# Decoder layer with 32 experts: order of experts computed at the last ranks, a 32-slot second expert, first down weights ahead of its gates, another tail

## The chip, the cores and the metric

The kernel runs on one core of a Trainium2 chip. The metric is the device time of one execution in microseconds (us), the median of the runs. The core's engines are PE (TensorE, matrix products into PSUM), DVE (VectorE), ACT (ScalarE), POOL (GpSimd) and SP (SyncE, here the queue that issues nearly all loads). They run side by side and wait for each other by semaphores; every engine works off its own instructions in the order in which they were written.

## The reference, cut to what matters

```python
def reference(x, positions, w_in, ..., w_gate_up, b_gate_up, w_down, b_down, ln2_g, ln2_b):
    mixed = attention(x) @ w_o[l]                      # two head groups, 512 tokens, width 1024
    x = layer_norm(DN_ALPHA * x + mixed, ln1_g[l], ln1_b[l])
    y = moe_ffn(x, w_router[l], b_router[l], w_gate_up[l], b_gate_up[l], w_down[l], b_down[l])
    x = layer_norm(DN_ALPHA * x + y, ln2_g[l], ln2_b[l])

def moe_ffn(...):
    logits = (xt @ w_router + b_router).astype(jnp.float32)
    top_logit, top_idx = lax.top_k(logits, TOP_K)      # 4 of 32 experts for each token
    gates = jax.nn.softmax(top_logit, axis=-1)
    ...
        h = xb @ w_gate_up[e] + b_gate_up[e]           # 1024 -> 2048
        act = (up + 1.0) * (gate * jax.nn.sigmoid(gate * SWIGLU_ALPHA))
        y = act @ w_down[e] + b_down[e]                # 1024 -> 1024
        return y * g[:, None]
```

All is float32. The weights of all 32 experts (12 MiB each, 384 MiB in all) are read whatever the router says.

## The kernel before

**Stages.** Projection and attention run over four blocks of 128 tokens (`PLAN`, `ORDER`, a table written by hand). A finished block goes through the `tasks`: output projection (`out_proj`), `norm` (layer norm, row block stored to `x1d`), `logits`, `logits2` (router) and `ranks`. `ranks` gives each token its place among the tokens of each expert (`rk1`). Then `moe` goes over 32 positions.

**Positions and kinds.** `KINDS` gives each position a kind: H has room for 128 tokens, L for 64, T for 32; G is H and T together, D is H and L. An H tile is split into two halves (`convert`: `whi` on ACT, `wlo` on DVE, lines 246 and 247) and multiplied in three passes (`mm3`, lines 253 to 255); the landed buffer is free again once it is converted. L and T use the landed tile itself (`mm_parts`, line 1261), with two or four pieces of the array side by side; the buffer is free once it has been multiplied. Positions 0 and 1 are both H and always hold experts 0 and 1, their weights have fixed addresses; which expert stands at a later position is computed (`permute`): experts by their count of tokens, the fullest in the positions with most room. The table `v` of experts is read into a register on SP (`expert_reg`) for the addresses of positions 2 and up.

**Weights.** `Stream` loads tiles of 1 MiB through SP into a ring of 11 buffers, 12 from the start of `moe`: eight gate/up tiles and four down tiles for each position. The work, and with it the order of the loads, is gates(0), gates(1), down(0), gates(2), down(1), and so on. A tile is loaded as soon as the program has released a buffer (`Stream.ahead`); when the engine that reads that buffer is late, SP waits there, and so does everything that it has to issue behind it.

**Start of `moe`.** The last call of `ranks` makes the matmul that selects the rows of expert 0 (`first_xT`: eight pairs, one on the gathered rows `xg` and one on the last block `x1`, lines 1165 and 1166). During gates(0) `permute` runs in pieces between the tiles (`between`), and so do the parts of the bias (`bias_part`). Rows for position 1 are gathered by POOL behind the loads of the biases, and turned to columns (`load_xT`) behind gates(0) and its `swiglu`.

**Tail.** Results of positions 0 to 29 are scattered to `yd`. Positions 30 and 31 are kept in SBUF and added by a matmul with the gates (`tail_kept`). While gates(31) run, `tail_y` loads the eight tiles of `yd` (two for each block of 128 tokens), ahead of the four down tiles of position 31. `tail_sum` adds four rows with their gates on DVE (line 1543), `tail_first` starts the sum of a block in PSUM (lines 1561 and 1551), `tail` ends with the layer norm and eight stores. In `down(31)` the blocks' `tail_first` stand between the four quarters.

## Time and profile before

| | us |
|---|---|
| median of 3 runs | 1410.86 |
| lowest and highest run | 1407.32, 1410.98 |
| the profiled execution, its own time | 1411.22 |
| span of its instructions | 1409.4 |

The span is read in four stretches: projection and attention (0 to about 314), the start of `moe` (314 to about 420), the row of experts (420 to about 1300) and the tail (1300 to the end). For each of them the rate of the DMA engines tells whether the weights come at full rate, and the waits tell who holds up whom. The engines' busy shares over the whole span (PE 91%) say little here, since they are means over stretches with different limits.

### The profile page before, as it was taken

To read this page: it belongs to the slowest core of one execution; us is meant where nothing else is said; L and a number is where in the kernel's file an instruction comes from. 1 tells how busy PE (TensorE), PEld (TensorE's weight loads), DVE (VectorE), ACT (ScalarE), POOL (GpSimd) and SP (SyncE) were. 2 spreads that over 40 slices of the span, in tenths; PEclk is the share of its full clock that TensorE was granted. 3 is DMA by queue.
4 is the path that set the end of the run, shared out by engine and by line. 5 is a ranking of instruction groups with operands and counts; after the bars stand their busy time and mean duration, and the time that the engine had idled before them with its cause. 6 is when DMAs were issued, how large, how long until landed. Compare 5 with 4: busy or idle time off the path is not lost.

```text
span 1409.4 us, 18034 instructions
## 1 busy us (share of the span) xinstructions
PE 1277.2 (91%) x6543; PEld 807.6 (57%) x6543; DVE 734.6 (52%) x1285; ACT 560.8 (40%) x829; POOL 162.8 (12%) x183
## 2 busy tenths in 40 slices
PE   6989697968999989999899999999999999999952
PEld 5767686856756435456554444647766556654310
DVE  4453654467946335335633523638855638752054
ACT  3442543335635224333622413536753627542201
POOL 2232100002001000010110000101011101000003
PEclk9999898979999999999999999999999999999887
DMA  9101730276799999999999998999999999999961
GB/s 336 72 1 60 273 146 34 90 281 239 290 375 415 416 418 418 413 413 416 417 417 415 416 353 349 417 417 416 417 417 417 417 413 414 415 415 408 407 261 65
DMA packets 92508, 464.70 MB, mean 330 GB/s; under 512 B 10226, under 2 KB 11426, under 8 KB 58624
## 3 DMA queue, kind: packets, MB, share of 16 engines
q1 hardware_dynamic: 82160, 435.42, 76.4%
q0 software_dynamic: 8000, 19.18, 3.8%
q10 hardware_dynamic: 2256, 8.91, 1.7%
q8 instruction: 53, 0.87, 0.2%
q14 instruction: 39, 0.32, 0.1%
HBM read 445.59 MB, written 25.03 MB: 334 GB/s over the span
## 4 chain that ended last, share of the span: by engine, by line
PE 55%; DMA 26%; DVE 9%; ACT 4%; issue 2%; POOL 1%; SPq 0%; ACTq 0%; DVEq 0%; POOLq 0%
PE acc L1261 14%; DMA raw<-in_w_down_dram 14%; DMA raw<-in_w_gate_up_dram 9%; PE acc L253 8%; PE acc L254 8%; PE acc L255 8%; DVE wlo L247 3%; PE acc L1267 2%; DMA yr<-yd 1%; PE ip L253 1%; PE ip L254 1%; PE ip L255 1%; DMA yr<-x1d 1%; PE po L667 1%; ACT whi L246 1%
## 5 line engine op out<-in xcount | busy, mean ns | idle before, releaser
L247 DVE TENSOR_TENSOR wlo<-raw,whi 128x1024 fp32r<-128x1024 f32 (+3 forms) x361 | 421.3, 1217 | 141.4 <-ACT whi L246 139.3
L246 ACT CAST whi<-raw 128x1024 fp32r<-128x1024 f32 (+3 forms) x361 | 358.4, 1046 | 175.4 <-DMA raw<-in_w_down_dram 81.1
L1261 PE MATMUL acc<-raw,xTs 128*64 128x512 f32 (+1 forms) x1280 | 266.8, 605 | 14.7 <-DMA raw<-in_w_gate_up_dram 14.6
L253 PE MATMUL acc<-whi,xTh 128*128 128x512 f32 x448 | 182.2, 407 | 0.7 <-ACT xTh L261 0.7
L254 PE MATMUL acc<-wlo,xTh 128*128 128x512 f32 x448 | 177.6, 396 | 0.6 <-DVE wlo L247 0.6
L255 PE MATMUL acc<-whi,xTl 128*128 128x512 f32 x448 | 177.4, 396 | 0.0
L1261 PEld LDWEIGHTS acc<-raw,xTs 128*64 128x64 f32 (+1 forms) x1280 | 71.6, 130 | 157.0 <-issue 119.5
L1372 POOL DMA_INDIRECT yd<-y,idx x34 | 52.8, 1552 | 675.5 <-ACT y L1360 458.0
L1261 PE MATMUL acc<-raw,aTs 128*64 128x512 f32 (+1 forms) x704 | 116.8, 525 | 14.3 <-DMA raw<-in_w_down_dram 14.3
L1309 DVE TENSOR_SCALAR u<-acc 128x512 f32<-128x512 f32 (+1 forms) x48 | 31.7, 660 | 163.5 <-ACT s L1308 163.5
L253 PEld LDWEIGHTS acc<-whi,xTh 128*128 128x128 f32 x448 | 84.4, 188 | 32.7 <-issue 9.1
L254 PE MATMUL acc<-wlo,aTh 128*128 128x512 f32 x224 | 90.4, 404 | 8.7 <-DVE wlo L247 8.6
L255 PEld LDWEIGHTS acc<-whi,xTl 128*128 128x128 f32 x448 | 84.3, 188 | 20.8 <-DVE xTl L262 0.4
L254 PEld LDWEIGHTS acc<-wlo,xTh 128*128 128x128 f32 x448 | 84.6, 189 | 19.8 <-DVE wlo L247 1.8
L1308 ACT ACTIVATE s<-acc 128x512 f32<-128x512 f32 (+1 forms) x48 | 27.6, 574 | 161.0 <-PE acc L1255 80.2
L253 PE MATMUL acc<-whi,aTh 128*128 128x512 f32 x224 | 90.2, 403 | 1.1 <-ACT whi L246 1.1
L1261 PEld LDWEIGHTS acc<-raw,aTs 128*64 128x64 f32 (+1 forms) x704 | 40.9, 129 | 86.5 <-issue 80.1
L255 PE MATMUL acc<-whi,aTl 128*128 128x512 f32 x224 | 89.2, 398 | 0.0
L1218 DVE SCALAR_TENSOR_TENSOR aTl<-tp,aTh 128x512 fp32r<-128x512 f32 x28 | 18.0, 686 | 111.0 <-ACT aTh L1214 110.8
L1197 POOL DMA_INDIRECT xg<-x1d,idx x34 | 40.9, 1204 | 291.9 <-issue 203.2
L1360 ACT COPY y<-acc 128x1024 f32<-128x1024 f32 (+2 forms) x32 | 23.7, 739 | 128.1 <-PE acc L255 66.8
L254 PEld LDWEIGHTS acc<-wlo,aTh 128*128 128x128 f32 x224 | 42.4, 189 | 22.9 <-DVE wlo L247 13.6
(324 smaller groups left out, 1558.0 us busy)
## 6 DMA issues: line engine op xcount, KB each, us to landing
raw<-in_w_gate_up_dram SPq DMA_DIRECT2D x256, 1024.0 KB, 19.9
raw<-in_w_down_dram SPq DMA_DIRECT2D x128, 1024.0 KB, 21.0
yd<-xg ACTq DMA_DIRECT2D x4, 2048.0 KB, 7.7
raw<-in_w_in_dram SPq DMA_DIRECT2D x6, 1024.0 KB, 15.5
raw<-yd SPq DMA_DIRECT2D x5, 1024.0 KB, 19.9
raw<-in_w_o_dram SPq DMA_DIRECT2D x4, 1024.0 KB, 4.9
yr<-yd SPq DMA_DIRECT2D x3, 1024.0 KB, 19.4
raw<-in_x_dram SPq DMA_DIRECT2D x4, 512.0 KB, 12.0
```

Of the source, the lines that this page charges most:

```text
L246: nc.scalar.copy(hi[:, js], t[:, js])
L247: nc.vector.tensor_tensor(lo[:, js], t[:, js], hi[:, js].bitcast(F32), op=ALU.subtract)
L253: nc.tensor.matmul(out, l[0], r[0], start=start, stop=False)
L254: nc.tensor.matmul(out, l[0], r[1], start=False, stop=False)
L255: nc.tensor.matmul(out, l[1], r[0], start=False, stop=stop)
L1197: nc.gpsimd.indirect_dma_start(out=B["xg"], out_offset=None, in_=self.rows(self.x1d, n), in_offset=bass.IndirectOffsetOnAxis(ap=B["idx"][: ...
L1261: self.nc.tensor.matmul(o[n * i:n * i + n], lT, r, start=start, stop=stop)
L1267: self.nc.tensor.matmul(o[n * i:n * i + n], self.blk[u[0], 0]["sel"][j].bitcast(F32)[:, :n], self.biasr.bitcast(F32)[:, c:c + w], start=st ...
L1308: nc.scalar.activation(s, ps[:, :w], AF.Silu, scale=SW)
L1309: nc.vector.tensor_scalar(u, ps[:, w:2 * w], LIM + 1.0, 1.0 - LIM, op0=ALU.min, op1=ALU.max)
L1360: nc.scalar.copy(y, B["d"])
L1372: self.nc.gpsimd.indirect_dma_start(out=self.rows(self.yd, n), out_offset=bass.IndirectOffsetOnAxis(ap=B["idx"][:, 1:2], axis=0), in_=y, i ...
```

## The change

Position 1 becomes a T, and the H that stood there moves to position 28, where three H now follow each other (26, 27, 28). Only position 0 keeps a fixed expert; the order is computed in the last `ranks` (`order_experts`), ahead of `moe`, and SP reads `v` from position 1 on. The four down tiles of position 0 are loaded ahead of the gates of position 1, and SP issues nothing beyond them until `v` is known (`hold`). `first_xT` is done in two halves, the first already in the last `norm`, into PSUM buffers of the attention (`sc`) that are given to the experts' sums only when `moe` has split them. Rows and indices of position 1 are picked by `columns` at the start of gates(0), its gather goes ahead of the bias loads, and its `load_xT` stands inside the last tile of gates(0). In the tail the sums of blocks 0 to 2 and their `tail_first` stand ahead of `down(31)`, the two last tiles of `yd` are loaded behind the weights of `down(31)`, and the statistics run two blocks ahead.

```diff
-KINDS = "HHTLHLLGLTHLHLLDLTHLHHTHLHLHHLLL"
+KINDS = "HTLHLLGLTHLHLLDLTHLHHTHLHLHHHLLL"
...
-        while self.nd < len(self.src) and kn.used < kn.limit and (most is None or self.nd <= most):
-            src, a, n, use = self.src[self.nd]
+        while self.nd < min(len(self.src), self.hold) and kn.used < kn.limit and (most is None or self.nd <= most):
+            i = self.order[self.nd] if self.order else self.nd
+            src, a, n, use = self.src[i]
...
+        order[n0 + 8:n0 + 20] = order[n0 + 16:n0 + 20] + order[n0 + 8:n0 + 16]
+        self.st.order, self.st.hold = order, n0 + 12
...
             def norm(q):
...
+                if len(ranked) == NT - 1:
+                    self.xT0 = [sc.tile([P, 512], F32, name="xT0", tag="sc") for _ in range(2)]
+                    self.first_xT(self.xg[0], self.ident, True)
...
             def ranks(q):
                 self.rank(q)
                 ranked.append(q)
-                if len(ranked) == NT:
+                if len(ranked) < NT:
+                    self.prep_tile((0, 0), q)
+                else:
                     mf = w.tile([P, P], F32, name="mf1", tag="pT", bufs=3)
                     nc.vector.tensor_scalar(mf, self.iob, self.rk1[:, q, 0:1], None, op0=ALU.is_equal)
-                for b in range(2):
-                    self.prep_tile((b, 0), q)
+                    ps = self.counts()
+                    self.first_xT(state.pop("x1"), mf, False)
+                    self.order_experts(ps)
+                    self.st.hold = len(self.st.src)
+                    self.st.ahead()
+                    self.prep_tile((0, 0), q)
...
-                if len(ranked) == NT:
-                    for b in range(2):
-                        self.prep2((b, 0))
-                    self.first_xT(state.pop("x1"), mf)
                 self.route2(q)
...
-        self.bias_load()
-        self.gather((1, 0))
+        self.scx.close()
+        self.pa = ctx.enter_context(tc.tile_pool(name="pa", bufs=3, space=PSUM))
...
+                if b == 0 and k == 0:
+                    self.pick_expert(1)
+                if b == 0 and k == 1:
+                    self.prep2((1, 0))
+                    self.gather((1, 0))
+                    self.bias_load()
+                if b == 0 and k == 2:
+                    self.prep2((0, 0))
...
+                if b == 0 and k == 7:
                     for _ in perm:
                         pass
+                    self.load_xT((1, 0))
                     self.prep((2, 0))
...
-            if b + 1 < E:
+            if 0 < b < E - 1:
                 for u in units(b + 1):
                     self.load_xT(u)
+            if b == KEPT[1]:
+                for t in range(NT - 1):
+                    self.tail_sum(t)
...
-        self.down(E - 1, self.tail_add)
+        self.tail_add()
+        self.down(E - 1)
...
+    def order_experts(self, ps):
+        nc.vector.tensor_copy(cc, ps[:, :E])
+        nc.vector.scalar_tensor_tensor(key, cc, float(E), self.c["keys"], op0=ALU.mult, op1=ALU.add)
+        pick(kcol, key, own)
+        nc.vector.tensor_scalar(gt, key, kcol, None, op0=ALU.is_gt)
+        nc.vector.tensor_reduce(rank, gt, axis=AX.X, op=ALU.add)
+        nc.vector.tensor_scalar(self.mt, self.c["rankpos"], rank, None, op0=ALU.is_equal)
+        ps = self.tp()
+        nc.tensor.matmul(ps[:, :E], self.c["ec"].to_broadcast([P, P]), self.mt, start=True, stop=True)
+        nc.vector.tensor_copy(self.v, ps[:, :E])
+        nc.vector.tensor_copy(self.vi, self.v[:1])
...
-        return w[b:b + 1] if b < 2 else w[bass.ds(self.expert_reg(b), 1)]
+        return w[b:b + 1] if b < 1 else w[bass.ds(self.expert_reg(b), 1)]
...
-    def tail_add(self, q):
-        if q == 0:
-            self.zp = {}
-            for t in range(NT):
-                self.tail_sum(t)
-        else:
-            self.tail_first(q - 1)
-        if q == 1:
-            B = self.blk[KEPT[0], 0]
-            self.scatter(B["y"], B, 2)
+    def tail_add(self):
+
+        B = self.blk[KEPT[0], 0]
+        self.blk[KEPT[1], 0]["room_d"] = self.acc()
+        self.zp = {}
+        for t in range(NT - 1):
+            self.tail_first(t)
+        self.tail_y(2 * NT)
+        assert len(self.ys) == 2 * NT
+        self.scatter(B["y"], B, 2)
+        self.tail_sum(NT - 1)
...
         stats(0)
+        stats(1)
         for t in range(NT):
-            if t + 1 < NT:
-                stats(t + 1)
+            if t + 2 < NT:
+                stats(t + 2)
             finish(t)
```

Three places show how the order moves. First SP's queue behind the last store to `x1d`; before, the loads go on through the gates of position 1 (fixed addresses), the four down tiles of position 0 and then `vi`, the table read for position 2:

```order
L739 DMA x1d<-z 128x1024
L158 DMA raw_2448<-in_w_gate_up_dram 128x2048
L158 DMA raw_2474<-in_w_gate_up_dram 128x2048
L158 DMA raw_2511<-in_w_gate_up_dram 128x2048
L158 DMA raw_2608<-in_w_gate_up_dram 128x2048
L158 DMA raw_2641<-in_w_gate_up_dram 128x2048
L158 DMA raw_2668<-in_w_down_dram 128x2x1024
L158 DMA raw_2693<-in_w_down_dram 128x2x1024
L158 DMA raw_2723<-in_w_down_dram 128x2x1024
L158 DMA raw_2751<-in_w_down_dram 128x2x1024
L1432 TENSOR_LOAD vi
```

The same place now:

```order
L161 DMA raw_2424<-in_w_down_dram 128x2x1024
L750 DMA x1d<-z 128x1024
L161 DMA raw_2458<-in_w_down_dram 128x2x1024
L1464 TENSOR_LOAD vi
L1464 ISA x2
L161 ISA
L161 DMA raw_2555<-in_w_gate_up_dram 128x2048
L161 ISA
L161 DMA raw_2566<-in_w_gate_up_dram 128x2048
```

The down tiles of position 0 have moved ahead, and SP reads `vi` before the first gate tile of position 1. Second, PE between the last ranks (`utb`) and the first product of position 0 (`acc`), before, where `tp` is the selected rows and the second line of each of the eight pairs takes the last block `z`:

```order
L1165 MATMUL tp<-cst,xg_1074 128x128
L1166 MATMUL tp<-mf_2519,z 128x128
L1165 MATMUL tp<-cst,xg_1074 128x128
L1166 MATMUL tp<-mf_2519,z 128x128
L253 MATMUL acc<-whi,xTh 128x512
```

And now, where `scr` is the scratch of the order of experts:

```order
L1071 LDWEIGHTS oneb
L1071 MATMUL tp<-sel,oneb 128x32
L1208 MATMUL xT_2446<-mf_2525,z 128x128 x4
L1208 MATMUL xT_2447<-mf_2525,z 128x128 x4
L1093 MATMUL tp<-scr,cst 128x32
L256 MATMUL acc<-whi,xTh 128x512
```

Eight of the sixteen products have left for an earlier place, and the counts and the order have come in. Third, PE in the tail, from the turned columns of position 31 (`tp<-cst,u`) on; `aTs` marks the products of `down(31)`, `mg` the kept positions:

```order
L1239 MATMUL tp<-cst,u 128x128 x4
L1267 MATMUL acc<-biasr,selw 64x512 x2
L1261 MATMUL acc<-raw_9806,aTs 64x512 x4
L1561 MATMUL acc<-yr,cst 128x512 x2
L1551 MATMUL acc<-y,mg 128x512 x2
L1261 MATMUL acc<-raw_9819,aTs 64x512 x4
L1561 MATMUL acc<-yr,cst 128x512 x2
L1551 MATMUL acc<-y,mg 128x512 x2
L1261 MATMUL acc<-raw_9836,aTs 64x512 x4
L1561 MATMUL tp<-yr,cst 128x512 x2
L1551 MATMUL tp<-y,mg 128x512 x2
L1261 MATMUL acc<-raw_9850,aTs 64x512 x4
```

Now:

```order
L1283 MATMUL tp<-cst,u 128x128 x4
L1594 MATMUL acc<-yr,cst 128x512 x2
L1584 MATMUL acc<-y,mg 128x512 x2
L1594 MATMUL acc<-yr,cst 128x512 x2
L1584 MATMUL acc<-y,mg 128x512 x2
L1594 MATMUL tp<-yr,cst 128x512 x2
L1584 MATMUL tp<-y,mg 128x512 x2
L1311 MATMUL acc<-biasr,selw 64x512 x2
L1305 MATMUL acc<-raw_9797,aTs 64x512 x4
L1305 MATMUL acc<-raw_9810,aTs 64x512 x4
L1305 MATMUL acc<-raw_9823,aTs 64x512 x4
L1305 MATMUL acc<-raw_9836,aTs 64x512 x4
```

The three blocks' sums have moved from between the quarters of `down(31)` to a place ahead of all four.

## Rows read from the trace of the kernel before

**Rows 1.** The page's GB/s of the DMA engines in 40 slices of 35.2 us:

```profile
GB/s 336 72 1 60 273 146 34 90 281 239 290 375 415 416 418 418 413 413 416 417 417 415 416 353 349 417 417 416 417 417 417 417 413 414 415 415 408 407 261 65
```

**Rows 2.** Windows: us, busy by engine, PE clock, DMA share, GB/s; last, gates(2), a T:

```profile
340.00:356.00 16.00, 9.13 (x42) 7.09 (x42) 13.30 (x16) 10.70 (x15) 0.00 (x0) 0.96 0.74 262
356.00:394.00 38.00, 38.00 (x176) 29.67 (x178) 31.65 (x51) 22.84 (x27) 3.20 (x2) 0.97 0.75 287
394.00:420.00 26.00, 26.00 (x168) 14.40 (x160) 12.99 (x26) 11.03 (x14) 3.08 (x3) 1.00 0.94 386
394.00:820.00 426.00, 410.44 (x2169) 217.27 (x2162) 196.20 (x311) 158.35 (x193) 38.30 (x31) 1.00 1.01 414
820.00:880.00 60.00, 59.02 (x278) 25.81 (x280) 18.41 (x32) 14.71 (x20) 3.35 (x3) 1.00 0.89 344
...
393.10:402.10 9.00, 9.00 (x87) 3.19 (x90) 3.68 (x11) 5.87 (x7) 2.06 (x2) 1.00 0.72 280
```

**Rows 3.** Waits of SP's queue, 340 to 400: who for whom, us, times, longest:

```profile
SPq L158 <- DVE wlo L247: 33.2, 10, 8.3
SPq L158 <- PE acc L1261: 5.9, 4, 4.7
```

**Rows 4.** Waits of SP's queue, 900 to 1200:

```profile
SPq L158 <- DMA raw<-in_w_down_dram: 75.3, 37, 3.3
SPq L158 <- DMA raw<-in_w_gate_up_dram: 71.6, 47, 2.0
```

**Rows 5.** SP's timeline (start, us, loads); then line 158's loads to landing, 340 to 420:

```profile
348.97 26.68 SPq L158 DMA_DIRECT2D raw<-in_w_gate_up_dram  x8
...
DMA to landing us min/median/max: 4.7/6.6/22.2
```

**Rows 6.** PE's timeline: first product of position 0, and its two waits after it:

```profile
322.05 0.50 PE L253 MATMUL acc<-whi,xTh 128*128 128x512 f32 x1 [0.72 <-ACT xTh L261]
345.37 0.71 PE L1100 MATMUL tp<-y 128*128 128x128 f32 x4 [2.57 <-ACT y L1095]
354.52 0.86 PE L1212 MATMUL tp<-cst,xg 128*128 128x128 f32 x4 [4.29 <-DVE xTl L1216]
```

**Rows 7.** Groups by line, 300 to 322: busy us, mean ns of one, idle before:

```profile
L1165 PE MATMUL tp<-cst,xg 128*128 128x128 f32 x16 | 5.0, 413 | 0.1
L780 ACT ACT_TABLE_LOAD x1 | 1.3, 1283 | 0.0
L749 ACT COPY x1T<-tp 128x512 f32<-128x512 f32 x2 | 1.2, 586 | 6.6 <-PE tp L747 6.6
L912 DVE TENSOR_SCALAR wk<-cst,ixf 128x32 bf16<-128x32 f32 x4 | 0.7, 236 | 0.0
```

**Rows 8.** Windows of gates(28) and down(27), both H; of gates(29), L, and down(28), H:

```profile
1214.80:1251.50 36.70, 36.70 (x168) 29.30 (x166) 29.61 (x41) 22.91 (x26) 2.31 (x2) 1.00 1.01 415
1251.50:1280.90 29.40, 29.40 (x141) 15.66 (x140) 12.99 (x17) 11.14 (x13) 2.04 (x2) 1.00 1.02 416
```

**Rows 9.** The chain that ended last (start, us): first of the four last loads:

```profile
1339.03 19.86 DMA raw<-in_w_down_dram
```

**Rows 10.** PE's timeline in the tail; last, the window ahead of it:

```profile
1359.03 3.27 PE L1261 MATMUL acc<-raw,aTs 128*64 128x512 f32 x8 [14.26 <-DMA raw<-in_w_down_dram]
1374.88 1.94 PE L1261 MATMUL acc<-raw,aTs 128*64 128x512 f32 x8
1382.44 1.99 PE L1551 MATMUL acc<-y,mg 64*128 64x512 f32 x8
...
1340.00:1360.00 20.00, 5.74 (x28) 1.89 (x26) 16.06 (x14) 0.97 (x2) 1.91 (x1) 0.70 0.95 391
```

**Rows 11.** DVE's and SP's timeline in the tail: sums, last norm, stores:

```profile
1351.75 12.92 DVE L1543 SCALAR_TENSOR_TENSOR yr<-raw,gates,yr 128x1024 f32<-128x1024 f32 x10
1395.59 0.98 DVE L1604 SCALAR_TENSOR_TENSOR yr<-yr,rs_t 128x512 f32<-128x512 f32 x1
1385.25 12.11 SPq L1606 DMA_DIRECT2D out_dram<-yr  x8
```

More of the change, by code (lines that the diff above doesn't have):

```diff
@@ L145, in __init__ @@
         self.nd = self.nc = self.at = 0
+        self.order, self.hold = None, 1 << 30
     def add(self, src, a, n, use=(True, False)):
@@ L957, in build @@
             self.xg = [self.me.tile([P, D], F32, name=f"xg{j}") for j in range(2)]
+            self.v = self.me.tile([P, E], F32, name="v")
+            self.vi = self.me.tile([1, E], I32, name="vi")
+            self.first = self.me.tile([P, 2], F32, name="first")
+            col = self.me.tile([P, 4], F32, name="pcol")
+            self.cnt, *self.pcol = (col[:, j:j + 1] for j in range(4))
             for j in range(2):
@@ L1043, in moe, with counts, pick @@
         self.tap("yd", self.yd)
+    def counts(self):
+        ps = self.tp()
+        for t in range(NT):
+            self.nc.tensor.matmul(ps[:, :E], self.oneb, self.sel[:, t], start=t == 0, stop=t == NT - 1)
+        return ps
+    def order_experts(self, ps):
+        nc = self.nc
+        scr = self.me.tile([P, 5 * E], F32, name="scr")
+        cc, key, gt, self.mt, junk = (scr[:, E * j:E * (j + 1)] for j in range(5))
+        kcol, rank, cap = self.pcol
+        own = self.c["e1"][:, :E]
+        def pick(out, row, by):
+            nc.vector.scalar_tensor_tensor(junk, row, 1.0, by, op0=ALU.mult, op1=ALU.mult, accum_out=out)
+        nc.vector.tensor_copy(cc, ps[:, :E])
[4 more added lines that the diff above has]
+        nc.vector.tensor_scalar(self.mt, self.c["rankpos"], rank, None, op0=ALU.is_equal)
+        ps = self.tp()
+        nc.tensor.matmul(ps[:, :E], self.c["ec"].to_broadcast([P, P]), self.mt, start=True, stop=True)
+        nc.vector.tensor_copy(self.v, ps[:, :E])
+        nc.vector.tensor_copy(self.vi, self.v[:1])
+        pick(self.cnt, cc, own)
+        pick(cap, self.mt, self.c["cappos"])
+        nc.vector.tensor_tensor(self.first[:, :1], cap, self.c["e1"][:, 32:33], op=ALU.add)
+        nc.vector.tensor_copy(self.first[:, 1:], self.c["e1"][:, 33:34])
@@ L1058, in permute @@
-        ps = self.tp()
+        nc.vector.tensor_copy(back.rearrange("p (t e) -> p t e", t=NT), arrays[1])
+        for j in range(2):
+            nc.vector.tensor_scalar(self.oh[:, j], self.v, self.c["pm"][:, j:j + 1], None, op0=ALU.is_equal)
         for t in range(NT):
-            nc.tensor.matmul(ps[:, :E], self.oneb, self.sel[:, t], start=t == 0, stop=t == NT - 1)
-        yield
-        own = self.c["e1"][:, :E]
-        def pick(out, row):
-            nc.vector.scalar_tensor_tensor(junk, row, 1.0, own, op0=ALU.mult, op1=ALU.mult, accum_out=out)
@@ L1156, in prep_sel, with first_xT @@
             self.nc.vector.tensor_scalar(B["sel"][j], self.oneb, oh, None, op0=ALU.mult)
[L1158 to L1161 removed]
+    def first_xT(self, rows, mf, start):
         for k in range(KD):
[L1163 to L1166 removed]
+            self.nc.tensor.matmul(self.xT0[k // 4][:, k % 4 * P:(k % 4 + 1) * P], rows[:, k * P:(k + 1) * P], mf,
+                                  start=start and k % 4 == 0, stop=not start and k % 4 == 3)
     def prep2(self, u, tiles=range(NT)):
@@ L1324, in swiglu, with down @@
         B["a"] = a[:, :FF // n]
-    def down(self, b, between=lambda q: None):
+    def down(self, b):
         for u in units(b):
```

149 lines of the change are left out of this document (59 added, 90 removed).

## The prediction

> **What bounds the kernel now.** I read the page's GB/s by slices first [rows 1]. From the thirteenth slice (about 420 us) almost to the end it stands at 413 to 418 in nearly all slices: there the weights set the pace, and a busy PE only keeps up. The waits of SP's queue say the same from the other side: between 900 and 1200 nearly all of SP's waiting ends with an earlier load that lands [rows 4]. Between 340 and 400 it is different: SP waits for the converter on DVE and for PE, so for a buffer of the ring [rows 3], and the rate is 262, 287 and 386 GB/s in three windows where 414 is to be had [rows 2]. The time thus falls into three pieces: when the stream reaches its full rate; how much it loses behind that (one place is seen, 820 to 880 at 344 GB/s [rows 2]); and how long the program runs behind the last landing. Only what changes one of these three counts.
>
> The profiled execution took 1411.22 us, its span 1409.4 with 1.8 around it, 0.4 above the median of the runs; the sum is made against 1411.2.
>
> **The front.** In the windows from 356 to 420 the stream loses 38 x (1 - 287/414) = 11.7 and 26 x (1 - 386/414) = 1.8, together 13.5 us [rows 2]. The cause is expert 1 as an H. Its tiles are converted at the rate of PE's twelve products for each, behind those of expert 0. As a T its eight gate tiles go through PE in about 9.0 us, as those of position 2 did [rows 2], 1.1 for a tile, and each frees its buffer at once. So from the first gate tile of position 1 on, the stream finds buffers.
>
> When is that? Up to there 20 tiles are loaded in both kernels (eight gates, eight gates, four down; in another order now), paced by the same conversions of expert 0. What moves is the start. Half of the sixteen selecting products leave the path: in the trace one group of them is busy for 5.0 us [rows 7] beside its twin, some 7 together, so about 3.5 are saved, in a place where PE had been idle. Added behind them are one product (0.4), eight small operations on DVE at 0.24 [rows 7] (1.9; the other five run beside the products), the exponential of the gates (0.5, an estimate by the small ones), the table load of 1.3 and its dummy, which lay beside the sixteen products and now come behind [rows 7], two copies of 0.6 and one subtraction of the same size (together 1.9, of which 0.9 stood there before). The last item is longer because the first product of position 0 now waits for both halves to be split: the PSUM that they stand in becomes its accumulator. Sum: -3.5 + 0.4 + 1.9 + 0.5 + 1.5 + 1.0, about 2 us later than 322.05 [rows 6]. PE has been idle for some 5 us there, so I add 1.5 for a start at the lower clock; the ends for this item are -1 and +6.
>
> Two waits go away behind it: 2.57 for the copy of `permute`, which is now written ahead of the conversions on ACT, and 4.29 at the change to position 1, whose columns were waiting behind conversions and `swiglu` on DVE [rows 6]; a T needs no subtraction and its columns are made inside the last tile of gates(0). The moved order of experts costs DVE nothing more during gates(0): `columns` comes in (about ten small operations, 2.4) and `permute`'s as many go out. So gates(1) begin at about 355 + 3.5 - 6.9 = 351.6 in place of 355, the first buffer is free at 352.7, and with 4.7 for a lone load [rows 5] tile 21 lands at 357.4. Before, tile 21 was issued at 348.97 [rows 5], so it landed at 353.7. The new stream is 3.7 behind there and at its full rate from there; the old one still had 13.5 to lose, and about 0.7 of the window before. **Front: 13.5 + 0.7 - 3.7, 10.5 us gained.** Ends: 4 (start and first T late by 6) and 13.5. The hold on SP costs nothing within that: `vi` is there at about 319, and nothing but those loads stands behind it; before, tiles 13 and 14 went out a little earlier, but the ring was full again in either case.
>
> **The row of experts.** Positions 1 to 27 are the old 2 to 28, so the D and its neighbours are unchanged and the loss at 820 to 880 comes one position earlier, equal in size: 60 x (1 - 344/414) = 10.1 us, before and after. New is H, H, H at 26 to 28. A position brings 12.6 MB and up to 1 MB of gathered and scattered rows, at 414 GB/s 31 to 33 us. Gates and down of two H take PE 36.7 [rows 8], so PE falls back by 4.5 for each such pair; an L with an H takes 29.4 [rows 8] and wins back 2.5. The change makes one such pair into two. In the old pair's window the stream kept 415 GB/s [rows 8], and 4.5 us are less than two of the ring's twelve tiles. I take no loss; the upper end is a second loss like the D's, 10.1. By the end of the row the three L have won back most of it.
>
> **The tail.** The last four weights land from 1339.03 + 19.86 = 1358.9 [rows 9], one each 1.05 MB/414 GB/s = 2.53 us, the last at E = 1366.5. From there it takes 42.9 to the end of the span: PE is done with `down(31)` at 1376.8 and with everything at 1384.4 (E + 18) [rows 10], DVE at 1396.6 (E + 30), SP's last store is issued at 1397.4, and 12 us are the store's landing and the program's end [rows 11]. In between PE spent its time in the wrong place: the three `tail_first` stood between the quarters, behind DVE's sums (1.29 each [rows 11]), the last of which ended at 1364.7.
>
> Now the same bytes are loaded, but the last to land is the second tile of block 3; call that E'. The weights of `down(31)` have landed at E' - 5, the sixth tile of `yd` at E' - 15. DVE has summed blocks 0 to 2 at E' - 12.5 (two sums, 2.6, behind that tile). PE then needs some 4 for the last `tail_first`, and 1 for the bias and 4 x 1.94 [rows 10] for `down(31)`: E' + 1 at the full clock. The two sums of block 3 end at E' + 2.6 and hold nobody up. Copy and last products take 7.6 as before (1376.8 to 1384.4): PE ends at E' + 9 to 10. Behind it DVE has the statistics of block 3 and three blocks to finish, about 8 (the old ending had 12.2, with blocks 0 to 2 finished one after the other, each waiting for POOL and ACT). Stores end at E' + 18.5 to 20 where they ended at E + 31. **Tail: 11 us gained**, ends 6 and 14. Covered at no cost: `y_keep` on ACT alone, longer by some 0.3.
>
> A first product behind a wait on a load takes longer here: eight took 3.27 at 1359.03, where a later eight took 1.94 [rows 10]; the window ahead had a granted clock of 0.70. The Trainium skill, "TensorE: Matmul & The Clock Gate", section "Loop structure matters more than you think", warns of this: matmuls that must wait between bursts let the PE go cold, and they then run at half rate. It speaks against the new order, where each `tail_first` waits for DVE. The trace agrees for the first products; whether the lower level would last through `down(31)` no row shows.
>
> **Sum.** 1411.2 - 10.5 - 11 = 1389.7; I say 1389.5.
>
> **Rivals.**
> 1. PE stays at 1.2 GHz from the last `tail_first` to the end of `down(31)`: the 7.8 and the 4 ahead take some 5 us longer. For it: PE is mostly idle while DVE sums. Against it: at 1359.03 the level rose within a few us of work. Time 1394.5. That is the rule of the section named above.
> 2. Three H in a row fill the ring and the stream loses 10.1, as at the D: 1399.5. Against it: 415 GB/s in the old pair [rows 8].
> 3. The front gains nothing, because the four down tiles hold a third of the ring through gates(0) and the start is late: 1400. For it: the wait for both halves. Against it: the conversions free the same buffers at the same times.
> 4. The tail gains nothing, since something in the new chain (the sums of block 3, POOL's additions) takes the place of PE: 1400.5. POOL needs about as long for three blocks as DVE, so this is possible in part.
> 5. What the front gains is lost at the three H, and the tail is as long as before; or the change does nothing that shows: 1411, within 0.3%.
> 6. Slower: PE's backlog at the three H outgrows the ring. Each further pair costs 4.5; from about 25 us of backlog (the ring's 30 less two tiles in flight) every tile waits for PE, the loads of `yd` wait for position 29's scatter, and the backlog's excess moves the end. The old pair reached some 12; it would have to double. Then two losses of the D's kind and the backlog itself, some 30 against the 21.5: 1419.
>
> An expert that no longer fits its position would add rounds of the overflow loop; that is excluded, since the positions' sizes are the same and one more expert is free to take the one that suits it.
>
> **How the numbers follow.** My forecast has 0.58 (its own range 1383 to 1397, from the ends of both terms, not all at once), rival 1 0.12, rival 2 0.08, rivals 3 and 4 0.06 each, rival 5 0.06, rival 6 0.04. The range of 8 in 10 reaches to rivals 2 to 4: 1382 to 1401. Faster by over 0.3% (4.2 us, about what a measurement of this kernel can tell from none) are all but 5 and 6: 0.90; same 0.06; slower 0.04.
>
> **What would show it.** Right: DMA at 410 GB/s or more from about 358, in place of 394 to 420; the first T product near 351; no wait of 4 us at the change to position 1; 413 GB/s through positions 26 to 28; 30 to 32 us from the last landing to the end of the span in place of 43. Wrong: a first product of position 0 later than 326, a new dip in GB/s near 1200, waits of SP for DVE or PE there, or PE's last product more than 12 us behind the last landing.

## The result, and the profile after

| kernel | median, us | before on the same chip | ratio, 95% interval |
|---|---|---|---|
| changed, first runs | 1396.73 (1388.50 to 1397.81) | 1410.92 | 0.9882 (0.9839 to 0.9925) |
| changed, unaltered, again | 1391.36 (1388.27 to 1397.05) | 1411.34 | 0.9853 (0.9835 to 0.9871) |

The medians of the changed kernel are 14 to 20 us lower, where 21.5 was forecast; 1396.73 lies within the range of 1382 to 1401. The execution whose trace is read took 1388.5 (span 1386.7), 8 us under its own median. The page's GB/s in 40 slices of 34.7 us, which answers to [rows 1]:

```profile
GB/s 332 83 1 61 277 137 47 94 232 269 405 415 416 416 415 416 412 415 415 415 416 416 348 360 402 414 416 417 415 416 416 413 414 407 410 397 415 411 356 71
```

The full rate starts one slice earlier. Windows of the changed kernel (columns as in [rows 2]; last, the place of the three H):

```profile
340.00:356.00 16.00, 14.45 (x120) 6.76 (x119) 11.40 (x27) 7.55 (x11) 2.10 (x2) 1.00 0.75 297
356.00:394.00 38.00, 38.00 (x231) 21.22 (x230) 18.01 (x33) 14.80 (x20) 3.60 (x3) 1.00 1.02 416
394.00:420.00 26.00, 26.00 (x123) 18.05 (x123) 17.50 (x30) 11.26 (x14) 1.30 (x1) 1.00 1.02 415
420.00:740.00 320.00, 304.92 (x1591) 156.00 (x1587) 137.32 (x219) 112.02 (x138) 26.55 (x23) 0.99 1.02 415
740.00:900.00 160.00, 157.31 (x815) 80.19 (x814) 68.33 (x105) 55.03 (x68) 12.58 (x11) 1.00 0.96 386
900.00:1200.00 300.00, 289.46 (x1419) 197.00 (x1418) 210.00 (x273) 169.27 (x197) 32.80 (x18) 0.99 1.02 414
...
1200.00:1250.00 50.00, 50.00 (x231) 36.60 (x229) 36.56 (x49) 30.12 (x34) 3.28 (x3) 1.00 1.00 400
```

416 and 415 stand where 287 and 386 stood [rows 2]. But the two traces can't be laid over each other as they are. The last store to `x1d`, the end of attention, is issued at different times; SP's timeline of before, of the changed kernel, and of its second trace:

```profile
305.72 0.33 SPq L739 DMA_DIRECT2D x1d<-z  x1
```

```profile
299.96 0.34 SPq L750 DMA_DIRECT2D x1d<-z  x1
```

```profile
307.78 0.34 SPq L750 DMA_DIRECT2D x1d<-z  x1
```

The stage before it is nearly the same code, and two executions of one kernel differ there by 7.8 us. Over all traces the store comes at 298.7 to 308.5 with the new front (eleven traces) and at 303.9 to 305.7 with the old one (three), so they show no shift by the change itself. Of the 22.7 us between the first two spans, 5.7 are this and not the change. So below all times are counted from that store, here called S, and the loads of weights are numbered from 0 in the order of their issue. The last landing is taken from the chain of waits (start and length of the last load, and 2.5 to 2.6 for each load behind the one named):

| kernel | S | first product | last landing | landing to end of span | S to end of span |
|---|---|---|---|---|---|
| before | 305.7 | 16.3 | 1061.0 | 42.7 | 1103.7 |
| before, again | 303.9 | 16.3 | 1061.4 | 44.1 | 1105.5 |
| changed | 300.0 | 17.0 | 1053.5 | 33.2 | 1086.7 |
| changed, again | 307.8 | 17.4 | 1054.3 | 33.2 | 1087.5 |

Counted so, the change gains 16.2 to 18.8: 6.7 to 7.9 up to the last landing and 9.5 to 10.9 behind it, according to which of the traces are compared.

PE's timeline at the start (answers to [rows 6]), and its waits from 314 to 400:

```profile
316.98 0.77 PE L256 MATMUL acc<-whi,xTh 128*128 128x512 f32 x1 [5.09 <-issue]
...
344.82 3.64 PE L1305 MATMUL acc<-raw,xTs 128*32 128x512 f32 x32
```

```profile
PE acc L256 <- issue: 5.1, 1, 5.1
PE tp L1283 <- DMA xg<-x1d,idx: 1.3, 1, 1.3
PE acc L1299 <- DVE biasr L1174: 0.2, 1, 0.2
```

The waits of 2.57 and 4.29 are gone; one of 1.3 on the gather of position 1 is new.

The tail, all engines (answers to [rows 10, 11]), and the end of the chain of waits:

```profile
1341.50 3.00 PE L1594 MATMUL tp<-yr,cst 128*128 128x512 f32 x4 [2.05 <-DVE yr L1576]
...
1347.03 7.04 PE L1305 MATMUL acc<-raw,aTs 128*64 128x512 f32 x32
...
1351.02 5.25 DVE L1576 SCALAR_TENSOR_TENSOR yr<-raw,gates,yr 128x1024 f32<-128x1024 f32 x4 [9.58 <-DMA raw<-yd]
...
1357.52 1.98 PE L1594 MATMUL acc<-yr,cst 128*128 128x512 f32 x4
...
1359.44 1.99 PE L1584 MATMUL acc<-y,mg 64*128 64x512 f32 x8
...
1363.51 2.93 POOL L1634 TENSOR_TENSOR yr<-yr 128x512 f32<-128x512 f32 x2
...
1363.87 4.33 DVE L1633 TENSOR_TENSOR yr<-yr 128x512 f32<-128x512 f32 x4
...
1368.32 5.83 POOL L1634 TENSOR_TENSOR yr<-yr 128x512 f32<-128x512 f32 x4
```

```profile
1334.99 18.49 DMA raw<-yd
1354.43 2.84 DMA yd<-y,idx
1363.55 2.89 POOL yr L1634 x2
1368.34 5.80 POOL yr L1634 x4
```

The last tile of `yd` lands at 1334.99 + 18.49 = 1353.5. `down(31)` is done at 1354.1 and PE at 1361.4, as forecast. But the chain ends on POOL: its six additions of `lnb2` run to 1374.15, 12.7 behind PE's last product. PE's end now is 7.9 behind the landing, where it was 17.7 (1384.4 [rows 10] less the landing at 1366.7); that is all of the gain, and from PE's end to the last work nothing was won (12.2 before).

### The profile page after: what moved, and what is told of

Read it like the earlier page. It is cut to its first block, busy times and chain, and to the rows that moved or that the text cites. A ratio compares the mean times of both kernels' runs of the same rounds, so it can differ in the third digit from the quotient of the medians.

```text
span 1386.7 us, 18062 instructions
## 1 busy us (share of the span) xinstructions
PE 1265.8 (91%) x6543; PEld 799.8 (58%) x6543; DVE 734.9 (53%) x1287; ACT 560.5 (40%) x829; POOL 159.6 (12%) x183
## 4 chain that ended last, share of the span: by engine, by line
PE 52%; DMA 26%; DVE 10%; ACT 3%; issue 3%; POOL 2%; SPq 1%; ACTq 0%; POOLq 0%; DVEq 0%
PE acc L1305 14%; DMA raw<-in_w_gate_up_dram 11%; DMA raw<-in_w_down_dram 11%; PE acc L256 7%; PE acc L257 7%; PE acc L258 7%; DVE wlo L250 5%; PE acc L1311 2%; DMA yr<-yd 1%; PE ip L256 1%; PE ip L257 1%; DMA raw<-yd 1%; PE ip L258 1%; PE zp L258 1%; PE zp L256 1%
## 5 line engine op out<-in xcount | busy, mean ns | idle before, releaser
L250 DVE TENSOR_TENSOR wlo<-raw,whi 128x1024 fp32r<-128x1024 f32 (+3 forms) x361 | 420.7, 1218 | 139.0 <-ACT whi L249 137.1
L249 ACT CAST whi<-raw 128x1024 fp32r<-128x1024 f32 (+3 forms) x361 | 358.7, 1048 | 178.9 <-DMA raw<-in_w_down_dram 78.6
L1305 PE MATMUL acc<-raw,xTs 128*64 128x512 f32 (+1 forms) x1280 | 263.1, 599 | 11.9 <-DMA raw<-in_w_gate_up_dram 11.5
L1414 POOL DMA_INDIRECT yd<-y,idx x34 | 50.0, 1470 | 669.2 <-ACT y L1403 480.5
```

Source lines behind the costliest of these rows:

```text
L249: nc.scalar.copy(hi[:, js], t[:, js])
L250: nc.vector.tensor_tensor(lo[:, js], t[:, js], hi[:, js].bitcast(F32), op=ALU.subtract)
L1305: self.nc.tensor.matmul(o[n * i:n * i + n], lT, r, start=start, stop=stop)
L1414: self.nc.gpsimd.indirect_dma_start(out=self.rows(self.yd, n), out_offset=bass.IndirectOffsetOnAxis(ap=B["idx"][:, 1:2], axis=0), in_=y, i ...
```

## The experiments

The theory after the traces: the T at position 1 gives what the front gains, the tail's order gives 9.5, and the 8 us between executions arise in attention. Rivals: the front's gain is the two waits of 2.57 and 4.29; the three H cost; the row of experts differs from chip to chip.

**The changed kernel again**, for a trace of a longer execution.

> The changed kernel once more, unaltered. Its first profiled execution took 1388.5 us, while three of four runs took 1395.7 to 1397.8, so the median of 1396.7 is 8 us above the execution whose trace is read. Span times mean granted clock is nearly the same for both kinds (1386.7 x 0.970 = 1345, 1396.0 x 0.963 = 1344). Theory 1: the difference is a stretch in which PE sets the pace and stood at the lower of its two levels, some 18 us of it (9 us of work at the full level), at the start of the moe stage or in the tail; then a trace of a longer execution shows the same DMA rate in the row of experts and that stretch longer. Theory 2: the stream of weights loses 8 us somewhere between 400 and 1300; then a window there shows under 400 GB/s where the first trace has 415. Either way the runs should again lie near 1388 and 1397, and the median at 1389 to 1397.

Five runs from 1388.27 to 1397.05. The profiled one took 1397.05, and 8.2 of its 8.5 us stand ahead of the first product: neither theory had that place. Windows in attention, the shorter execution and the longer:

```profile
232.00:240.00 8.00, 3.15 (x21) 2.34 (x19) 4.11 (x9) 3.15 (x13) 1.41 (x3) 0.78 0.39 132
240.00:250.00 10.00, 9.75 (x74) 9.44 (x75) 5.30 (x28) 4.73 (x15) 0.00 (x0) 0.84 0.00 1
250.00:262.00 12.00, 11.88 (x84) 10.74 (x84) 5.55 (x16) 5.54 (x18) 1.41 (x3) 1.00 0.42 156
```

```profile
232.00:240.00 8.00, 5.04 (x42) 4.58 (x40) 5.63 (x12) 2.90 (x11) 0.74 (x2) 1.00 0.10 37
240.00:250.00 10.00, 7.41 (x35) 6.87 (x35) 2.43 (x8) 3.27 (x11) 1.40 (x3) 0.57 0.22 77
250.00:262.00 12.00, 11.88 (x84) 11.62 (x84) 7.33 (x31) 4.39 (x14) 0.00 (x0) 0.79 0.01 1
```

Both wait for ACT at the same instruction for the same 3.2 us. In the first the granted clock falls to its lower level (1.2 GHz) during the wait and is back early; in the second it falls behind it and stays down into 255 while PE has work (0.57 and 0.79). The same over the whole stretch up to S:

```profile
0.00:299.96 299.96, 250.89 (x1429) 216.38 (x1429) 153.63 (x404) 116.11 (x290) 51.40 (x88) 0.95 0.38 139
0.00:307.78 307.78, 259.04 (x1429) 224.19 (x1429) 153.95 (x404) 115.74 (x290) 51.29 (x88) 0.93 0.37 136
```

300.0 x 0.95 = 285.0 and 307.8 x 0.93 = 286.2: time at the lower level makes up most of the 7.8 us between these two traces. Over all traces the same product still differs by some 5 us, so about half of the whole spread has another source that no run shows.

**The kernel before again.**

> The kernel before, unaltered, for a second trace of it. Counted from the issue of the last store to x1d (the end of attention, 305.7 in the first trace), the last weight landed at 1061.0 and the span ended at 1103.7; from the landing of load 45 to that of load 375 it took 888.7 us, where three traces of kernels with the new front took 893.7 to 894.0 and the one of the old front with the new tail took 892.1. Theory 1: the changed kernel's row of experts is itself 5 us slower, and takes back part of what its front gains; then this trace shows 888 to 890 again. Theory 2: the row's rate differs from execution to execution or chip to chip, and the first trace of before was a good one; then it shows 891 to 894, a last landing at 1063 to 1066, and the change gains that much more than the two first traces say.

Between the issues of the same two gate tiles (the first of position 6 and the first of position 28; in the changed kernel positions 5 and 27) the two traces of before take 710.6 and 710.7, the two of the changed kernel 712.9 and 713.1. Counted from S, the issues of the loads agree in the two traces of before to 0.9 us, nearly all to 0.5, from load 12 to the last. So theory 1. The changed kernel's row is 2.3 us slower for the same work. S to the end is 1105.5: the old tail took 1.4 us longer here.

**The two halves of the change.** `tail_only` is the kernel before with all of the diff's tail, `front_only` the changed kernel without it. The cut goes through the main loop so:

```diff
+            if b == KEPT[1]:
+                for t in range(NT - 1):
+                    self.tail_sum(t)
...
-        self.down(E - 1, self.tail_add)
+        self.tail_add()
+        self.down(E - 1)
```

> The kernel before with the new tail alone (sums and first products of blocks 0 to 2 ahead of down(31), two last tiles of yd behind its weights, statistics two blocks ahead, y_keep on ACT alone); front and kinds as before. By the prediction the tail gives 11 us: 1400. By the traces of before and after it gives 7.0: from the last landing to the end of the span 1409.4 - 1366.7 = 42.7 before, 1386.7 - 1351.0 = 35.7 after; then 1404 for an execution like the one profiled of before. Rival: the tail gives nothing by itself and what moved is the front: 1411, with the last landing still at 1366 and 42 us behind it.

1402.36 against 1411.34: 0.9938 (0.9919 to 0.9958). 33.2 from the last landing to the end, as in the changed kernel; but the landing itself is at S + 1064.5, 3.5 later than before, and the two tiles are 713.8 apart, in a stretch that no line of this kernel changes. What differs there is the addresses of the buffers, since its small tiles for the tail take more room (see the ring's addresses below). Which of the tail's three parts (sums ahead, two tiles of `yd` last, statistics two blocks ahead) gives how much was not separated.

> The changed kernel with the old tail; so order, second position, loads and starts are new. By the prediction the front gives 10.5: 1400.5. By the traces the last landing came 15.7 earlier (1366.7 to 1351.0): 1395.5, and 42 to 43 us from the last landing to the end of the span. If the 8 us between executions of the changed kernel come from the front, runs of this one spread by as much; if from the tail, they do not, and those of the kernel with the new tail alone do.

1404.30 against 1411.34: 0.9946 (0.9927 to 0.9966). Last landing at S + 1053.9, the changed kernel's; 42.7 behind it, the old tail's. Each part is there without the other: 7.1 counted to the landing, 9.5 counted from it. The medians gain 9.0 and 7.0, less than the 20.0 of the whole change against the same runs of before, in part by the 3.5 that `tail_only` loses in the row. This kernel's seven runs spread by 8.8 with the old tail, so the spread is not the tail's.

**The three H parted.**

```diff
-KINDS = "HTLHLLGLTHLHLLDLTHLHHTHLHLHHHLLL"
+KINDS = "HTLHLLGLTHLHLLDLTHLHHTHHLHLHHLLL"
```

> The changed kernel with the H of position 28 put at position 22, so that three pairs of H stand where a pair and a triple stood; positions 0 to 21 and 28 to 31 otherwise alike, same number of each kind. In the trace of the changed kernel the lead of the stream over the kernel before falls from 15.9 us (load 230) to 13.5 (load 362) around the three H, and the window 1200 to 1250 shows 400 GB/s. If the triple costs that, this one is 2 us faster: 1386.5 beside 1388.5, no window of 50 us between 1100 and 1300 under 410 GB/s. If the loss is one of any pair (PE falls behind by 4.5 us in each), it stays or moves: 1388.5. If the H gets in the way of the L and T around position 22, slower by 2 to 4.

1395.06 against 1411.34: 0.9876 (0.9845 to 0.9907). S to end 1087.2, last landing at S + 1054.0: nothing gained. The loss moves to other windows:

```profile
1150.00:1200.00 50.00, 49.52 (x234) 34.29 (x233) 34.55 (x43) 28.84 (x33) 6.38 (x3) 1.00 1.01 407
1200.00:1250.00 50.00, 50.00 (x230) 33.67 (x228) 36.93 (x49) 29.09 (x34) 3.28 (x3) 1.00 1.01 414
1250.00:1300.00 50.00, 50.00 (x238) 22.84 (x238) 16.27 (x29) 13.48 (x17) 2.02 (x2) 1.00 1.00 406
```

By the issue of load 360 its lead over the kernel before is 7.4 us where the changed kernel has 3.6; by that of load 372 the two have 7.3 and 7.7. What the triple loses is won back by the three L.

**Position 1 an H again.**

```diff
-KINDS = "HTLHLLGLTHLHLLDLTHLHHTHLHLHHHLLL"
+KINDS = "HHTLHLLGLTHLHLLDLTHLHHTHLHLHHLLL"
...
-                    self.load_xT((1, 0))
                     self.prep((2, 0))
...
-            if 0 < b < E - 1:
+            if b < E - 1:
```

> The changed kernel with position 1 an H again (kinds as before, a pair of H at 27 and 28; its columns are turned behind gates(0), as a T's place inside the last tile has no room for a pair); order of experts, loads, first columns and tail stay new. By the prediction the T is the whole reason for the front's gain: 12.4 us at load 45 in the traces. Then that gain falls to 0 or a little below, since the later start (0.6 to 1.0) stays, and the time is 9 to 12 above the changed kernel: 1401 to 1406. Rival: part of the gain is from the copy of permute and the earlier columns, two waits of 2.57 and 4.29 before; then 4 to 7 of the 12 stay at load 45, and the time is 1396 to 1400.

1407.05 against 1411.36: 0.9958 (0.9939 to 0.9977); S to end 1098.5, 11.4 above the changed kernel. At load 44 it is 1.1 behind the kernel before. Its windows at S + 40, S + 56 and S + 94:

```profile
348.00:364.00 16.00, 11.51 (x48) 8.65 (x48) 14.80 (x25) 10.94 (x14) 1.82 (x1) 0.89 0.72 276
364.00:402.00 38.00, 38.00 (x198) 28.19 (x200) 27.91 (x40) 22.45 (x27) 2.35 (x2) 1.00 0.83 311
402.00:428.00 26.00, 26.00 (x150) 14.10 (x152) 12.47 (x28) 9.50 (x12) 2.04 (x2) 1.00 1.01 411
```

The pause of the stream is back (276 and 311). But the rival isn't quite excluded, since two waits at this place are back as well:

```profile
PE acc L1298 <- DVE biasr L1173: 3.0, 2, 2.7
PE tp L1217 <- DVE xTl L1258: 1.5, 1, 1.5
```

4.5 us of waits stand where 6.9 stood before and 1.5 in the changed kernel. What the run shows is that the T, together with the early columns that only a T has room for, gives all of the front's gain, and that order, loads and first columns give nothing without it. How the 12 us divide between the buffers and the waits is not shown.

**Loads in the order of use.**

```diff
-        order[n0 + 8:n0 + 20] = order[n0 + 16:n0 + 20] + order[n0 + 8:n0 + 16]
-        self.st.order, self.st.hold = order, n0 + 12
+        self.st.order, self.st.hold = order, n0 + 8
```

> The changed kernel with the loads in the order of use: the four down tiles of position 0 behind the gates of position 1, and SP held behind the eight gates of position 0 until the order of experts is known. Four loads less can go out ahead of that point (13.5 us behind the last store to x1d). Theory 1: the ring's buffers set the pace through gates(0), the four loads are made up for while it is converted, and nothing is lost: last landing at 1053 to 1055 behind that store, 1389 to 1397 like the changed kernel. Theory 2: the four loads are lost to the stream, 4 x 2.53 = 10 us: 1399 to 1407.

1398.76 against 1411.36: 0.9918 (0.9898 to 0.9937). S to end 1090.4, 3 above the changed kernel, between the theories. Load 20 goes out at the same time, load 32 too; the 3 us are lost behind them, by load 44. Why they are lost there is open.

**The additions left out.**

```diff
-                    nc.gpsimd.tensor_tensor(z[:, ns], z[:, ns], self.lnb2[:, ns], op=ALU.add)
```

> The changed kernel without the six additions of lnb2 on POOL at the end of blocks 0 to 2 (left out, not moved; the outputs of these blocks lack that term). From the last landing to the end of the span the changed kernel takes 33.2 us in both traces; its DVE ends 10.4 behind PE's last product, POOL 12.8. Theory 1: POOL's additions (1.46 each, with the three small steps of block 3 between them) are what ends last, where the prediction had DVE; then 33.2 becomes 29 to 31, with DVE last. Theory 2: the statistics and multiplications on DVE and ACT set the end and POOL only follows; then it stays at 32.5 to 33.2.

One run, 1388.50 with S at 304.8: 27.6 from the last landing to the end, 5.6 less: theory 1, and more than expected. DVE is now last, 7.8 behind PE's last product, and its four multiplications take 0.61 each, not 1.08:

```profile
1369.56 2.44 DVE L1633 TENSOR_TENSOR yr<-yr 128x512 f32<-128x512 f32 x4
...
1374.22 0.75 DVE L1637 SCALAR_TENSOR_TENSOR yr<-yr,rs_t 128x512 f32<-128x512 f32 x1
```

So POOL's work ended last, and slowed DVE beside it. That is what the Trainium skill, "SBUF — State Buffer", section "Who interferes with whom", says of a DVE instruction with two inputs in SBUF beside a GpSimd one that reads there; 0.61 and 1.08 agree with it.

**The additions on PE and ACT.**

```diff
+                nc.tensor.matmul(self.zp[t][n], self.ident, self.lnb2[:, ns], start=True, stop=False)
+                nc.tensor.matmul(self.zp[t][n], self.ident, z[:, ns], start=False, stop=True)
+                nc.scalar.copy(z[:, ns], self.zp[t][n])
```

> The changed kernel with the six additions of lnb2 in blocks 0 to 2 moved from POOL to PE and ACT (two products of the unit matrix into the block's PSUM, lnb2 and the scaled rows, then a copy on ACT and the store). With the additions left out the time from the last landing to the end of the span was 27.5 us in place of 33.2, DVE last. PE is idle there; a pair of products is about 1 to 2 us by the rows of tail_first, a copy on ACT 0.6. Theory 1: what cost was POOL and its work beside DVE's; then it takes 27.5 to 29.5. Theory 2: the longer way through PE and ACT (three engines for each half) takes the place of POOL; then 31 to 34. The median is lower than the changed kernel's by 4 to 5 or by nothing, seen through a spread of 8 us between runs.

1395.51 against 1411.12, 0.9884 (0.9854 to 0.9915); 35.0 from landing to end, 1.8 more than with POOL: theory 2. Each half goes through PE and ACT one after the other, the last two copies 1.7 apart:

```profile
1380.00 0.59 ACT L1648 COPY yr<-acc 128x512 f32<-128x512 f32 x1 [2.07 <-PE acc L1647]
...
1381.72 0.59 ACT L1648 COPY yr<-tp 128x512 f32<-128x512 f32 x1 [1.13 <-PE tp L1647]
...
1383.43 0.59 ACT L1648 COPY yr<-tp 128x512 f32<-128x512 f32 x1 [1.13 <-PE tp L1647]
```

**PE kept at work in attention.**

```diff
+                    if g == 1 and len(ranked) == 1:
+                        idle = sc.tile([P, 512], F32, name="idle", tag="sc")
+                        for _ in range(18):
+                            nc.tensor.matmul(idle[:, :384], self.oneb, self.maskw[:, :384], start=True, stop=True)
```

> The changed kernel with 18 products of constants (bf16, 384 columns, results not used) on PE between the two groups of turned columns of the second finished block, where PE waits 3.17 us for ACT in every trace. In the traces the issue of the last store to x1d lies between 298.7 and 308.5 us, although that stage is the same code; PE's work around 240 ran at the lower level for some 6 us where it came at 300.0 and for some 14 where it came at 307.8. Theory 1: that wait lets the clock fall, and how long it stays down differs from execution to execution; with PE kept at work the granted clock stays at 0.9 or above from 232 to 260, the last store to x1d comes at 296 to 301, and the runs lie within 3 us of each other near 1386 to 1389. Theory 2: the spread has another place (the waits around 150, 285 or 305), or the products come too late to hold the level; then the runs still spread from 1388 to 1397.

Five runs from 1385.78 to 1393.97, median 1391.27 against 1411.12 (0.9849, 0.9826 to 0.9872): the spread is still 8 us, S at 304.9. The products fill the wait (0.25 is left of 3.2); PE's timeline:

```profile
234.85 3.09 PE L762 MATMUL idle<-maskw,oneb 128*128 128x384 bf16 x18
238.19 0.66 PE L765 MATMUL tp<-cst,z 128*128 128x128 f32 x4 [0.25 <-ACT pT L665]
240.31 0.71 PE L676 MATMUL po<-raw,pT 128*128 128x128 f32 x4 [1.46 <-DVE mix L695]
241.78 0.47 PE L663 MATMUL tp<-cst,e 128*128 128x128 f32 x2 [0.76 <-ACT x1T L767]
```

The granted clock falls none the less, behind the waits of 1.46 and 0.76; the windows:

```profile
232.00:240.00 8.00, 5.92 (x42) 4.08 (x40) 4.11 (x10) 3.33 (x13) 1.73 (x4) 1.00 0.37 129
240.00:250.00 10.00, 8.93 (x44) 8.74 (x45) 4.17 (x20) 3.27 (x9) 0.00 (x0) 0.60 0.01 4
250.00:262.00 12.00, 11.88 (x95) 11.54 (x95) 6.71 (x22) 5.32 (x16) 0.00 (x0) 0.90 0.02 6
```

Theory 1 falls. What decides how long PE stays at 1.2 GHz there is open.

**The ring's addresses.** The row's 2 to 3 us had no place yet. The ring's first eleven buffers begin at byte 74272 of a partition in the kernel before and in `front_only`, at 74464 in the others: 32 beyond a multiple of 64 in all. One unused piece of 32 bytes moves them, and the split tiles in front of them, to 74496; a second one keeps the gathered rows at 32 beyond a multiple of 64:

```diff
+        ctx.enter_context(tc.tile_pool(name="pad1", bufs=1)).tile([P, 8], F32, name="pad1")
         self.hp = ctx.enter_context(tc.tile_pool(name="hilo", bufs=3))
...
+            ctx.enter_context(tc.tile_pool(name="pad2", bufs=1)).tile([P, 8], F32, name="pad2")
             self.me = ctx.enter_context(tc.tile_pool(name="me", bufs=1))
```

> The changed kernel with two unused pieces of 32 bytes per partition, which move the eleven buffers of the ring and the split tiles from an address of 32 beyond a multiple of 64 to a multiple of 64, nothing else. Between the same two tiles (first gates of before's position 6 and of its position 28) the kernel before takes 710.6 and 710.7 us, all changed ones 712.1 to 714.2, the one with the new tail alone 713.8 too; the buffers' addresses differ among them. Theory 1: the address of a buffer sets a few parts in a thousand of the stream's rate; then this one takes 710 or less, or clearly more than 714. Theory 2: it does not; then 712 to 714.

1378.61 in one run: 701.4 between the two tiles, S to end 1070.6, 16 to 17 us less than the changed kernel. Windows of it:

```profile
420.00:740.00 320.00, 307.07 (x1618) 157.92 (x1616) 139.47 (x227) 112.59 (x140) 28.09 (x23) 1.00 1.02 423
740.00:900.00 160.00, 158.33 (x824) 81.62 (x821) 70.22 (x107) 56.87 (x73) 12.56 (x11) 1.00 0.96 389
900.00:1200.00 300.00, 290.57 (x1440) 199.70 (x1440) 214.05 (x277) 172.16 (x199) 32.23 (x18) 1.00 1.01 422
```

423 and 422 where the changed kernel has 415 and 414. The same with the gathered rows moved too:

```diff
             self.xg = [self.me.tile([P, D], F32, name=f"xg{j}") for j in range(2)]
+            self.me.tile([P, 8], F32, name="pad2")
```

> The changed kernel with the ring's buffers and the split tiles at a multiple of 64 bytes, as in the run before it, and the two buffers of gathered rows there too (xg0, xg1 were 32 beyond one in all kernels so far). The first move alone gave 701.4 us between the two tiles where 710 to 714 stood, 423 GB/s where 415 stood, and a last landing 1037.4 behind the last store to x1d in place of 1053.5. Theory 1: only the stream's own buffers count; then 700 to 702 again, 1036 to 1039, and with that store at 299 to 308 the runs lie between 1371 and 1381. Theory 2: the gathered rows (half a megabyte for a position) gain too: 697 to 700, and 1 to 3 us less. If the first run was a lucky one, this one is back at 712 and at 1388 to 1397.

1379.62 (1374.14 to 1380.89) against 1410.53: **0.9770 (0.9748 to 0.9791)**, the fastest of all. 701.3 between the tiles and 1070.8 from S to the end: the gathered rows' address adds nothing. The split tiles moved with the buffers in both runs, but splitting took as long as ever (1218 ns apiece on DVE in the changed kernel and 1216 in `aligned`, 1048 and 1047 on ACT), so the gain is put down to the loads themselves.

One buffer is left out of this: the twelfth, which joins the ring at the start of `moe`. In the kernel before it begins at byte 206592, a multiple of 256; in `tail_only` it is 192 beyond one, in `front_only` and in both aligned kernels 128, in the changed kernel 64. So before is the only kernel that had one buffer of twelve at a multiple of 256 and eleven beside one.

## Why the prediction was right, point by point

**The bound** was read rightly: what counted was when the stream reaches its full rate, what it loses behind that, and what runs behind the last landing. `front_only` and `tail_only` divide the gain as those pieces say. Two signs came out a little beside the forecast: 400 GB/s in a window at the three H, and 33.2 us from the last landing to the end, not 30 to 32.

**The start** was put 2 us later and 1.5 more for the clock; the first product came 0.7 to 1.1 later. The first T product stands at S + 44.9 (45.9 in the forecast), the issue of load 20, the prediction's tile 21, is 2.7 behind the kernel before (3.7 in the forecast).

**The T**, with the early columns that it allows, is the front's gain, as said: `second_H` loses all of it. By the landing of load 45 the stream is 12.3 ahead (11.8 in the second trace), where 10.5 was forecast; 1.0 of the difference is the start, for which too much was put.

**The row** is the step that failed in size: "I take no loss". By landings, the lead falls from 12.3 at load 45 to 7.3 at load 375, with ups and downs between, since the two kernels have different kinds at the same load. It isn't the triple H: `no_triple` lands at the same time, so rival 2's loss of 10.1 isn't there either. Between the two tiles of equal work the loss is 2.3. The rest of the 5 lies outside them, where the order of the kinds differs, and no run divides it. For the 2.3 there is a suspect that no run tried alone. `tail_only` loses 3.2 between the same tiles with the kinds and the code of before, and `front_only` 2.5 though its first eleven buffers lie where those of before do. Both differ from before in the twelfth buffer, which is no longer at a multiple of 256, as in the changed kernel. The size doesn't quite fit: eleven moved buffers gained 11.6 between these tiles in `aligned`, so one gains 1.1 by estimate. So the address may be the cause of a part, and the cause as a whole stays open.

**The tail** was put at 11 and gives 9.5 (10.9 against the second trace of before). The sums of blocks 0 to 2 end 12.1 ahead of the last landing (12.5 in the forecast), `down(31)` 0.6 behind it (1), PE 7.9 (9 to 10). Then the mis-sized term: "DVE has the statistics of block 3 and three blocks to finish, about 8" is 12.7, since POOL comes last. Without POOL's additions it is 7.8 with DVE last, so the term was right for DVE and left POOL out. The prediction named POOL in rival 4 and took it for a draw with DVE; it is slower, and slows DVE. That the sum is off by 1.5 only is in part luck. By the issue of the last store, which the forecast counted, the new tail ends 22.0 behind the landing (18.5 to 20) and the old one 30.6 (31), which is 8.6; another 0.9 came from what lies behind that issue, 12.0 before and 11.2 now, where the forecast had it equal.

**Rival 1**, PE at the lower level through `down(31)`: no. 32 products took 7.04, so 1.76 for eight, under the 1.94 of [rows 10]. The products that wait for DVE did run slowly (3.00 for four, where four later ones took 1.98), which cost nothing that the chain shows: the chain goes through POOL's scatter behind the last landing, and the first block's statistics (done at 1357.7) wait for POOL until 1359.1.

**The sum**, counted from S: 21.5 forecast, 16.2 to 18.8 measured. The predicted 1389.5 is close to the profiled 1388.5 only because that execution had 5.7 us of luck in attention; with S where it was in the trace of before the changed kernel would have taken 1394 to 1395, and the median of 1396.73 is 7 above the forecast.

## What to carry to other kernels

Before two traces are subtracted, count both from a mark behind the last stage that the change leaves alone; else a stage that varies by itself is booked as gain. In a stream of weights, the tile that holds its buffer longest sets the restart: here one expert that needs no conversion was worth 11 us at the right place, and three that do in a row cost nothing where lighter ones follow. Where DMA sets the pace, look at the buffers' addresses before the order of work: 32 bytes gave 16 us here, about as much as the whole change.

## What the runs showed of the hardware that was not expected

- The rate of the loads goes by the address of their buffers: 414 to 416 GB/s with eleven of the ring's twelve at 32 or 224 beyond a multiple of 256, 422 to 423 with the eleven at a multiple of 256 (74496 = 291 x 256), in the traces of two kernels and the times of six runs. Whether 64, 128 or 256 is what counts was not tried. The Trainium skill, "DMA: Bandwidth & Descriptors", section "How a descriptor splits into AXI transactions", says that a descriptor which doesn't begin at a multiple of 256 bytes costs transfers for bytes that aren't used. The runs agree for 0 against the rest. By that account, as an estimate, a start 224 beyond would waste seven times as much as one 32 beyond; the runs don't show that (between the two tiles 713.1 in `front_only` at 32, 712.9 in the changed kernel at 224).
- The same stage of the same program ended between 298.7 and 308.5. With the granted clock at 0.84 in one window (0.95 over the stage) S was 300.0, with 0.57 (0.93) it was 307.8; 3 us of products put into the longest wait did not hold the higher level.
- An addition of 128x512 on POOL takes 1.46 us, and multiplications on DVE 1.08 beside it, 0.61 without.
